# Three of four pairs of the pooling branch's gates made from products of blocks, in a two-layer decoder trunk on one core

## The chip, the cores and the metric

The kernel runs on one core of a Trainium2 chip. Its time is that of one execution on the device, in microseconds; the time of a kernel is the median of its runs. A profile is taken of one further execution. The engines are named as the profile names them: PE multiplies matrices (PEld is its loading of weights), DVE, ACT and POOL work element by element, SP issues transfers (POOL issues some, too).

## What is computed

Two layers, 512 tokens of 1024 features, float32. Each layer has a retention branch and a pooling branch that are merged with gates, then a SwiGLU feed-forward part (FFN). Cut to what matters here:

```
for l in range(DEPTH):                                     # 2
    h = modulate(rmsnorm(x, norm1[l]), sh1, sc1)
    proj = h @ w_in[l]
    q, k, v, g_sw, p_in, gates = jnp.split(proj, IN_SPLITS, axis=-1)
    ...
    ret_d = (jax.nn.silu(g_sw) * ret) @ w_ret_o[l]
    pool_d = (pooled * pool_scale[l]) @ w_pool_o[l]
    a_ret, a_pool = jnp.split(gates, N_BRANCH, axis=-1)
    merged = jax.nn.sigmoid(a_ret) * ret_d + jax.nn.sigmoid(a_pool) * pool_d
    x = x + g1[:, None, :] * (merged @ w_out[l])
    h2 = modulate(rmsnorm(x, norm2[l]), sh2, sc2)
    gate, up = jnp.split(h2 @ w_ffn_in[l], 2, axis=-1)
    x = x + g2[:, None, :] * ((jax.nn.silu(gate) * up) @ w_ffn_out[l])
```

The six modulation vectors of a layer come from `c` and `w_ada`.

## The kernel before, in words

*Layout and precision.* Everything is kept transposed: features on the 128 partitions, the 512 tokens along the row. A tile of 128 features of `h` is therefore 128x512, and `KT` = 8 of them make `h`. Each float32 operand is split into a rounded part and a residue (`hi` and `lo`, both in a reduced float32 type), and `mm3` makes one product from three matmuls: hi by hi, lo by hi, hi by lo. So a column of 128 outputs over all 8 tiles of `h` takes 8 x 3 = 24 matmuls of 512 columns (`project`, line 590).

*Weights.* All weights lie in one stream, `wst`, in chunks of 8 units of 128x128 (512 KB), in the order in which the program asks for them (the table `order`). `ahead(c)` (line 565) prepares chunk c and the two behind it. `prep` (line 504) loads a chunk into one of 3 `raw` tiles and splits it into two of 11 `w` tiles: a copy that rounds (DVE or ACT), and either a subtraction (DVE or POOL) or, for about half of the chunks, a negated copy on ACT and a second transfer that adds the chunk to it (a POOL transfer). The modulation tiles of `w_ada` pass the same 3 `raw` tiles, `background()` (line 634) takes the next of them: one load, and one DVE instruction that multiplies and sums.

*Blocks.* In the FFN, 8 of the 22 pairs of a gate column and an up column (`SEVEN`) are made as a 2 x 2 product of blocks with 7 products of blocks and sums of blocks instead of 8: the two columns are one side, the two halves of the 8 tiles of `h2` the inner side, the two halves of the tokens the other. Each product has 256 columns. `seven_chunk` (line 524) lays the 16 units of a pair into two chunks; `seven_prep` (line 533) loads such a chunk, makes four sums of weight blocks on DVE (256 columns each, into two tiles `r` of 512), and splits the chunk (768 columns of it) and the two tiles of sums: four `w` tiles in all. The sums of `h2` are made once for a layer, into eight pair tiles (`x`). `seven(i)` (line 1047) issues the 84 matmuls into four PSUM tiles (there are 8), and combines these with a copy on ACT and five additions on DVE.

A chunk enters the table `sevens` when its pair is recorded. `ahead` of an earlier column may have reached it before, and has then prepared it as an ordinary chunk; `seven_prep` loads it again.

*The branches.* The retention branch's end (the loop at line 980) goes over 8 columns j: 24 matmuls for the gate, sigmoid, 24 for `ret_o`, the product of the two kept in `m_`, and one modulation tile. The pooling branch's end (line 999) does the same with 24 matmuls for its gate and 12 for `pool_o` (4 tiles of `pooled`), adds `m_[j]`, splits the sum for `w_out`, and takes two modulation tiles. Then come `w_out`'s 8 columns, the second norm, and the FFN.

*What sets the order.* Operations are recorded first (`Recorder`). PE keeps the recorded order; the others are ordered by the times that a planner (`Recorder.order`, line 277) reckons for each engine, by when the result is due, and by when a tile of a pool comes free. `nc.either` leaves the choice of DVE or POOL to it, `copy` that of ACT or DVE. Each engine then runs its list strictly in that order. All instructions are issued at line 421, so a profile tells them apart by the names of their tiles.

Of the kernel before, what the change touches and what calls it, by code (L numbers as in the profile page):

```python
# [14 lines left out]
P = 128  # L15
D = 1024
# [49 lines left out]
SEVEN = [set(range(5, FT - 1, 2))] * DEPTH  # L66
HALF_KT = KT // 2
# [365 lines left out]
def trunk(ctx, tc, xT, cin, wada, vecs, wst, rot, trid, icnt, out):  # L433
# [156 lines left out]
    def project(o, l, name, col, src, sl=FULL, k0=0, mid=None):  # L590
        n = len(src)
        for k in range(n):
            if mid and k == n // 2:
                mid()
            mm3(o[:, sl], unit(l, name, k0 + k, col), hs(src[k], sl), k == 0, k == n - 1)

# [261 lines left out]
    for l in range(DEPTH):  # L858
# [119 lines left out]

        m_ = []
        for j in range(KT):  # L980
            o = ps()
            project(o, l, "in", C_A + j * P, h, mid=head_norm)
            sg = temp()
            nc.scalar.activation(sg, o, AF.Sigmoid)
            while fill:
                filler()
            rp = ps()
            project(rp, l, "ret_o", j * P, y)
            m = keep(F32)
            nc.vector.tensor_mul(out=m, in0=rp, in1=sg)  # L990
            m_.append(m)
            background()
# [3 lines left out]
        for g in (3, 2, 1, 0):  # L996
            group(g)
        pooled = [p2[g] for g in range(4)]
        for j in range(KT):
            gp = ps()  # L1000
            project(gp, l, "in", C_A + D + j * P, h)
            sg = temp()
            nc.scalar.activation(sg, gp, AF.Sigmoid)
            rp = ps()
            project(rp, l, "pool_o", j * P, pooled)
            t = temp()
            nc.vector.tensor_mul(out=t, in0=rp, in1=sg)
            nc.vector.tensor_add(out=t, in0=t, in1=m_[j])
            merged.append(split(t))
            background(2)  # L1010
# [21 lines left out]
        while len(order) % UNITS:  # L1032
            order[("none", len(order))] = len(order)
        done = first_tiles(l, 2, h2, "ffn_in", [0, FF, P], norm_b, block)
        for k in range(HALF_KT):
            t13, t24 = temp(), temp()
            b11, b21, b12, b22 = (block(kk, n) for n, kk in ((0, k), (0, k + HALF_KT), (1, k), (1, k + HALF_KT)))
            nc.either.tensor_sub(out=t13[:, A], in0=b12, in1=b11)
            nc.either.tensor_sub(out=t13[:, B], in0=b12, in1=b22)
            nc.either.tensor_sub(out=t24[:, A], in0=b22, in1=t13[:, A])  # L1040
            nc.either.tensor_sub(out=t24[:, B], in0=b21, in1=t24[:, A])
            hi, lo = sums[k]
            for n, t in enumerate((t13, t24)):
                copy(hi[:, n], t)
                nc.either.tensor_sub(out=lo[:, n], in0=t, in1=hi[:, n].bitcast(F32))

        def seven(i):

            cs = [seven_chunk(l, i, k0) for k0 in (0, 2)]
            o = [ps() for _ in range(4)]  # L1050
            for k in range(HALF_KT):
                ahead(cs[k // 2])
                if k % 2:
                    continue
                (ah, al), (sh, sl) = sevens[cs[k // 2]]

                for (wh, wl), n, bank, at, act in (
                    ((ah, al), 0, 0, 0, "b11"), ((ah, al), 1, 1, 0, "b21"), ((ah, al), 2, 3, 1, 3),
                    ((sh, sl), 2, 1, 1, 2), ((sh, sl), 3, 2, 0, 0), ((sh, sl), 0, 2, 1, 1), ((sh, sl), 1, 3, 0, "b22"),
                ):  # L1060
                    for d in range(2):
                        ws = slice((2 * n + d) * P, (2 * n + d + 1) * P)
                        if isinstance(act, str):
                            a = hs(h2[k + d + HALF_KT * (act[1] == "2")], A if act[2] == "1" else B)
                        else:
                            a = tuple(z[:, act // 2, act % 2 * 256:act % 2 * 256 + 256] for z in sums[k + d])
                        first = k + d == 0 and (bank, at) in ((0, 0), (1, 0), (3, 1), (2, 0))
                        last = k + d == HALF_KT - 1 and (bank, at) in ((0, 0), (1, 1), (2, 1), (3, 0))
                        mm3(o[bank][:, at * 256:at * 256 + 256], (wh[:, ws], wl[:, ws]), a, first, last)
            m1 = temp()[:, A]  # L1070
            nc.scalar.copy(out=m1, in_=o[0][:, A])
            gate, up, u = temp(), temp(), temp()
# [127 lines left out]
```

## Time and profile before

| | us |
|---|---|
| median of 3 runs | 1537.04 (1536.17 to 1537.6) |
| profiled execution: its own time | 1535.18 |
| its span (first to last instruction) | 1533.0 |
| PE, waits for other engines in total | 21 |
| DVE busy | 1006.4 |

The granted clock of PE is full from 100 us on. 286.77 MB are moved in all, 187 GB/s on average. The page's list of DMA issues counts 295 loads of a chunk on SP (4.5 us from issue to landing in the median), 129 on POOL that add to a `w` tile, and 96 loads of modulation tiles on SP.

How to read the rows further on: a timeline row is the start, the time from the first start to the last end of a run of like instructions, the engine, the line, the operation, the tiles (output, arrow, inputs; `w` weights, `h` parts of h or h2, `x` sums of blocks, `r` other activations, `ps` PSUM, `t` temporaries), the shapes and the count; in brackets stands the idle time ahead of it and what ended it. Since matmuls overlap a little, the pace of a stream is read from start to start.

### The profile page before, as it was taken

The numbers are of one execution on the slowest core, as the hardware profiler recorded it, in microseconds if no ns is written. First come the engines' busy times: TensorE is split into PE (matmuls) and PEld (weight loads), VectorE is DVE, ScalarE is ACT, GpSimd is POOL, SyncE is SP. The second block draws the span as 40 slices with busy tenths as digits, with TensorE's granted clock in tenths as the row PEclk, the third lists the DMA queues.
The fourth block names the chain that finished last, engine by engine and source line by source line (L and its number), as shares of the span: only waits on it lengthen the run. The fifth ranks groups of instructions, "written<-read, shape, count | busy, mean of one in ns | idle before, by whom it ended". The sixth has DMA issues, their size and how long they took to land. (4 is left out here: it accounts for less than half of the span.)

```text
span 1533.0 us, 20526 instructions
## 1 busy us (share of the span) xinstructions
PE 1503.3 (98%) x7878; PEld 1287.2 (84%) x7878; DVE 1006.4 (66%) x1650; ACT 645.7 (42%) x912; POOL 300.5 (20%) x291
## 2 busy tenths in 40 slices
PE   7999999999999999999999999999999999999997
PEld 5788888888888888998888888888889888899887
DVE  8877684465568957885366768535647696478633
ACT  2377552322464412342267766322227433243332
POOL 0023151011142300222011312101211432012101
PEclk8999999999999999999999999999999999999999
DMA  7857738789694684559487865777897757444553
GB/s 259 269 158 190 161 74 255 190 246 283 149 234 153 200 251 158 170 169 279 118 221 166 202 149 134 201 180 230 251 232 182 203 167 218 124 130 159 165 125 83
DMA packets 82788, 286.77 MB, mean 187 GB/s; under 512 B 9217, under 2 KB 11521, under 8 KB 82690
## 3 DMA queue, kind: packets, MB, share of 16 engines
q1 hardware_dynamic: 64114, 217.82, 42.5%
q0 software_dynamic: 18576, 67.64, 25.1%
q8 instruction: 61, 1.00, 0.3%
q14 instruction: 37, 0.30, 0.1%
HBM read 283.33 MB, written 2.10 MB: 186 GB/s over the span
## 5 line engine op out<-in xcount | busy, mean ns | idle before, releaser
L421 PE MATMUL ps<-h,w 128*128 128x512 f32 (+1 forms) x3888 | 793.4, 362 | 8.6 <-DVE h L421 5.2
L421 PEld LDWEIGHTS ps<-h,w 128*128 128x128 f32 x3888 | 659.1, 189 | 126.2 <-DVE h L421 6.4
L421 PE MATMUL ps<-r,w 128*128 128x512 f32 (+1 forms) x2430 | 476.8, 356 | 0.1
L421 PEld LDWEIGHTS ps<-r,w 128*128 128x128 f32 x2430 | 402.3, 188 | 69.1 <-DVE r L421 0.9
L421 ACT CAST w<-raw 128x1024 fp32r<-128x1024 f32 (+2 forms) x181 | 183.3, 1013 | 346.9 <-DMA raw<-wst 190.3
L421 DVE TENSOR_TENSOR w<-raw,w 128x1024 fp32r<-128x1024 f32 (+2 forms) x162 | 206.4, 1276 | 102.5 <-PE ps L421 71.7
L421 POOL DMA_DIRECT2D w<-wst x129 | 113.6, 881 | 743.6 <-ACT w L421 690.8
L421 ACT ACTIVATE w<-w 128x1024 fp32r<-128x1024 f32 x129 | 136.6, 1060 | 200.6 <-issue 75.6
L421 DVE CAST w<-raw 128x1024 fp32r<-128x1024 f32 (+2 forms) x115 | 80.4, 699 | 169.0 <-PE ps L421 95.4
L421 DVE SCALAR_TENSOR_TENSOR raw<-raw,cact 128x1024 f32<-128x1024 f32 x96 | 122.5, 1280 | 35.0 <-DMA raw<-wada 33.9
L421 PE MATMUL ps<-x,w 128*128 128x256 f32 x768 | 96.2, 280 | 2.1 <-DVE w L421 2.1
L421 PEld LDWEIGHTS ps<-x,w 128*128 128x128 f32 x768 | 92.8, 188 | 2.5 <-DVE w L421 2.5
L421 PE MATMUL ps<-w,h 128*128 128x512 f32 x384 | 90.3, 395 | 0.0
L421 POOL TENSOR_TENSOR r<-t,r 128x512 fp32r<-128x512 f32 x48 | 79.8, 1669 | 41.1 <-ACT r L421 29.4
L421 PEld LDWEIGHTS ps<-w,h 128*128 128x128 f32 x384 | 72.0, 188 | 17.8 <-ACT r L421 0.4
L421 DVE SCALAR_TENSOR_TENSOR xall<-ps,mod,xall 128x512 f32<-128x512 f32 (+1 forms) x62 | 38.6, 629 | 72.6 <-PE ps L421 72.6
L421 ACT CAST r<-t 128x512 fp32r<-128x512 f32 (+1 forms) x106 | 65.2, 618 | 33.7 <-DVE t L421 25.7
L421 ACT ACTIVATE t<-ps 128x512 f32<-128x512 f32 x76 | 44.9, 593 | 77.8 <-PE ps L421 77.8
L421 DVE TENSOR_TENSOR t<-ps,t 128x512 f32<-128x512 f32 x76 | 51.9, 684 | 15.5 <-PE ps L421 14.6
L421 ACT COPY t<-ps 32x512 f32<-32x512 f32 (+2 forms) x88 | 47.2, 539 | 30.2 <-PE ps L421 20.6
L421 ACT ACTIVATE t<-xall 128x256 f32<-128x256 f32 (+1 forms) x44 | 21.2, 492 | 81.8 <-DVE xall L421 81.5
L421 PE MATMUL ps<-x,r 128*128 128x256 f32 (+2 forms) x256 | 52.7, 323 | 0.0
(93 smaller groups left out, 973.6 us busy)
## 6 DMA issues: line engine op xcount, KB each, us to landing
raw<-wst SPq DMA_DIRECT2D x295, 512.0 KB, 4.5
w<-wst POOLq DMA_DIRECT2D x129, 512.0 KB, 7.5
raw<-wada SPq DMA_DIRECT2D x96, 512.0 KB, 4.8
x<-rot SPq DMA_DIRECT2D x32, 256.0 KB, 7.3
xall<-xT SPq DMA_DIRECT2D x4, 512.0 KB, 5.2
out<-t SPq DMA_DIRECT2D x7, 256.0 KB, 2.2
out<-t SPq DMA_DIRECT2D x2, 128.0 KB, 2.1
tri<-trid SPq DMA_DIRECT2D x1, 128.0 KB, 4.9
```

The costliest lines, as they stand in the source:

```text
L421: getattr(eng, method)(*[real(a) for a in args], **{k: real(v) for k, v in kw.items()})
```

## The change

The pooling branch's gate columns are taken in pairs. Pair 0 (columns 0 and 1) is made as before; pairs 1, 2 and 3 are made by blocks, with the code that was in `seven`, now `block_products`. Behind each pair come its two `pool_o` columns. The sums of h (`make_gate_sums`) are recorded in the first four columns of the retention branch, into the eight pair tiles. The chunks of all block pairs, those of the FFN too, are entered in `sevens` ahead of the columns whose look-ahead reaches them, so that none is prepared as an ordinary chunk first. For that the stream is filled up to a whole chunk ahead of the pooling gates, no longer ahead of the FFN. `seven_prep` makes its three rounding copies on ACT. Of the modulation tiles, two go with each column of the retention branch and one with each of the pooling branch.

```diff
+BLOCK_RET, BLOCK_POOL = (), (1, 2, 3)
...
-    def seven_chunk(l, i, k0):
+    def seven_chunk(l, name, c0, c1, k0):
         c = len(order) // UNITS
-        assert len(order) % UNITS == 0
-        for k, col in ((0, 0), (HALF_KT, 0), (HALF_KT, FF), (0, FF)):
+        assert len(order) % UNITS == 0 and c in sevens
+        for k, col in ((0, c0), (HALF_KT, c0), (HALF_KT, c1), (0, c1)):
             for d in range(2):
-                order[(l, "ffn_in", k + k0 + d, col + i * P)] = len(order)
-        sevens[c] = None
+                order[(l, name, k + k0 + d, col)] = len(order)
         return c
...
-        copy(ah[:, :3 * w], af[:, :3 * w])
+        nc.scalar.copy(out=ah[:, :3 * w], in_=af[:, :3 * w])
...
-            copy(sh[:, part], sf)
+            nc.scalar.copy(out=sh[:, part], in_=sf)
...
+    def block_sums(k, b11, b21, b12, b22, to):
+
+        t13, t24 = temp(), temp()
+        nc.either.tensor_sub(out=t13[:, A], in0=b12, in1=b11)
+        nc.either.tensor_sub(out=t13[:, B], in0=b12, in1=b22)
+        nc.either.tensor_sub(out=t24[:, A], in0=b22, in1=t13[:, A])
+        nc.either.tensor_sub(out=t24[:, B], in0=b21, in1=t24[:, A])
+        hi, lo = to
+        for n, t in enumerate((t13, t24)):
+            copy(hi[:, n], t)
+            nc.either.tensor_sub(out=lo[:, n], in0=t, in1=hi[:, n].bitcast(F32))
+
+    def block_products(l, name, c0, c1, h, sums):
+
+        cs = [seven_chunk(l, name, c0, c1, k0) for k0 in (0, 2)]
+        o = [ps() for _ in range(4)]
...
+        m1 = temp()[:, A]
+        nc.scalar.copy(out=m1, in_=o[0][:, A])
+        gate, up, u = temp(), temp(), temp()
+        nc.vector.tensor_add(out=gate.halves(), in0=o[1].halves(), in1=m1.twice())
+        nc.vector.tensor_add(out=u.halves(), in0=o[2].halves(), in1=gate[:, B].twice())
+        nc.vector.tensor_add(out=gate[:, B], in0=u[:, A], in1=o[3][:, A])
+        nc.vector.tensor_add(out=up[:, A], in0=u[:, B], in1=o[3][:, B])
+        nc.vector.tensor_add(out=up[:, B], in0=u[:, B], in1=o[2][:, A])
+        return gate, up
...
+        for n in BLOCK_POOL:
+            sevens[base + 17 + 3 * n] = sevens[base + 18 + 3 * n] = None
+        gate_sums = [(pair_tile(F32R), pair_tile(F32R)) for _ in range(HALF_KT)]
+
+        def make_gate_sums(k):
+            w = [temp() for _ in range(2)]
+            for t, z in zip(w, (h[k], h[k + HALF_KT])):
+                nc.either.tensor_add(out=t, in0=z[0].bitcast(F32), in1=z[1].bitcast(F32))
+            block_sums(k, w[0][:, A], w[1][:, A], w[0][:, B], w[1][:, B], gate_sums[k])
+
+        def branch(j0, by_blocks, c, mid=None):
+
+            if by_blocks:
+                o = block_products(l, "in", c + j0 * P, c + j0 * P + P, h, gate_sums)
+                for t in o:
+                    nc.scalar.activation(t, t, AF.Sigmoid)
+                yield from enumerate(o, j0)
+                return
...
+                background(2)
+                if j < HALF_KT:
+                    make_gate_sums(j)
...
+        while len(order) % UNITS:
+            order[("none", len(order))] = len(order)
         pooled = [p2[g] for g in range(4)]
...
+        for n in range(HALF_KT):
+            for j, sg in branch(2 * n, n in BLOCK_POOL, C_A + D):
+                rp = ps()
+                project(rp, l, "pool_o", j * P, pooled)
...
+                background()
...
-        while len(order) % UNITS:
-            order[("none", len(order))] = len(order)
+        assert len(order) % UNITS == 0
+        for i in SEVEN[l]:
+            c = len(order) // UNITS + 2 * i + sum(i1 - i0 for i0, i1 in zip(FF_CUTS, FF_CUTS[1:]) if i1 <= i)
+            sevens[c] = sevens[c + 1] = None
```

Where the change moves instructions, first PE, at gate column 2 of layer 0's pooling branch, ahead of it the last product of `pool_o`'s column 1. Before:

```order
L421 MATMUL ps_2685<-r_2608,w_2483 128x512
L421 MATMUL ps_2706<-h_199,w_2483 128x512
L421 MATMUL ps_2706<-h_199,w_2515 128x512
L421 MATMUL ps_2706<-h_222,w_2483 128x512
L421 MATMUL ps_2706<-h_250,w_2483 128x512
L421 MATMUL ps_2706<-h_250,w_2515 128x512
L421 MATMUL ps_2706<-h_307,w_2483 128x512
```

And now, where `w_2600` and `w_2651` are the parts of the chunk itself, with the waits in brackets:

```order
L423 MATMUL ps_2784<-r_2687,w_2575 128x512
L423 MATMUL ps_2811<-h_199,w_2600 128x256
L423 MATMUL ps_2811<-h_199,w_2651 128x256 [waits Pool_49]
L423 MATMUL ps_2811<-h_222,w_2600 128x256
L423 MATMUL ps_2811<-h_250,w_2600 128x256
L423 MATMUL ps_2811<-h_250,w_2651 128x256
L423 MATMUL ps_2811<-h_307,w_2600 128x256
L423 MATMUL ps_2820<-h_410,w_2600 128x256
L423 MATMUL ps_2820<-h_410,w_2651 128x256
```

After two of the eight tiles of `h` the stream goes on to another PSUM tile with other weights of the same chunk; ahead of it the order of PE is that of before. Second, DVE of the changed kernel at the end of pair 1 in the same branch: `raw_2765` is the second chunk of pair 2, `w_2877`, `w_2907` and `w_2947` are residues of pair 2's weights, `ps_2820`, `ps_2852` and `ps_2834` the products of pair 1:

```order
L423 TENSOR_TENSOR w_2877<-r_2786,w_2846 128x512 [waits Activation_49]
L423 TENSOR_TENSOR t_2814<-t_2814,r_2135 128x512
L423 TENSOR_TENSOR w_2907<-raw_2765,w_2880 128x768 [waits PE_49,Activation_49]
L423 TENSOR_TENSOR t_2919<-ps_2820,t_2892 128x512 [waits PE_49,Activation_49]
L423 SCALAR_TENSOR_TENSOR raw_2859,mod_0_150<-raw_2859,cact_73 128x1024 [waits DMAHW0_49,DVE_49]
L423 TENSOR_TENSOR w_2947<-r_2832,w_2914 128x512 [waits PE_49,Activation_49]
L423 TENSOR_TENSOR w_2947<-r_2823,w_2914 128x512 [waits DVE_49,Activation_49]
L423 TENSOR_TENSOR t_2960<-ps_2852,t_2919 128x512 [waits DVE_49,Pool_49]
L423 TENSOR_TENSOR t_2919<-t_2960,ps_2834 128x256 [waits DVE_49,PE_49]
L423 TENSOR_TENSOR t_2969<-t_2960,ps_2834 128x256
```

At that place DVE had one addition and split of a column and two modulation tiles before; now the residues of the next pair stand among the combination of this one, and those of `raw_2765` wait for PE to free their tiles. Third, SP in the second half of layer 0's FFN, from one modulation tile (`wada`) to the next. Before:

```order
L421 DMA raw_5900<-wada 128x1024
L421 DMA raw_5941<-wst 128x1024
L421 DMA raw_5966<-wst 128x1024
L421 DMA raw_5980<-wst 128x1024
L421 DMA raw_6023<-wst 128x1024
L421 DMA raw_6074<-wst 128x1024
L421 DMA raw_6109<-wst 128x1024
L421 DMA raw_6133<-wada 128x1024
```

And now:

```order
L423 DMA raw_5661<-wada 128x1024
L423 DMA raw_5693<-wst 128x1024
L423 DMA raw_5755<-wst 128x1024
L423 DMA raw_5771<-wst 128x1024
L423 DMA raw_5842<-wst 128x1024
L423 DMA raw_5873<-wada 128x1024
```

Two of six loads in each such period are gone.

More of the change, by code (lines that the diff above doesn't have):

```diff
@@ new lines, in block_products @@
+    def block_products(l, name, c0, c1, h, sums):
+        cs = [seven_chunk(l, name, c0, c1, k0) for k0 in (0, 2)]
+        o = [ps() for _ in range(4)]
+        for k in range(HALF_KT):
+            ahead(cs[k // 2])
+            if k % 2:
+                continue
+            (ah, al), (sh, sl) = sevens[cs[k // 2]]
+            for (wh, wl), n, bank, at, act in (
+                ((ah, al), 0, 0, 0, "b11"), ((ah, al), 1, 1, 0, "b21"), ((ah, al), 2, 3, 1, 3),
+                ((sh, sl), 2, 1, 1, 2), ((sh, sl), 3, 2, 0, 0), ((sh, sl), 0, 2, 1, 1), ((sh, sl), 1, 3, 0, "b22"),
+            ):
+                for d in range(2):
+                    ws = slice((2 * n + d) * P, (2 * n + d + 1) * P)
+                    if isinstance(act, str):
+                        a = hs(h[k + d + HALF_KT * (act[1] == "2")], A if act[2] == "1" else B)
+                    else:
+                        a = tuple(z[:, act // 2, act % 2 * 256:act % 2 * 256 + 256] for z in sums[k + d])
+                    first = k + d == 0 and (bank, at) in ((0, 0), (1, 0), (3, 1), (2, 0))
+                    last = k + d == HALF_KT - 1 and (bank, at) in ((0, 0), (1, 1), (2, 1), (3, 0))
+                    mm3(o[bank][:, at * 256:at * 256 + 256], (wh[:, ws], wl[:, ws]), a, first, last)
+        m1 = temp()[:, A]
[7 more added lines that the diff above has]
+        return gate, up
@@ L997, in trunk @@
             group(g)
+        while len(order) % UNITS:
+            order[("none", len(order))] = len(order)
         pooled = [p2[g] for g in range(4)]
[L999 to L1010, printed above, removed]
+        for n in range(HALF_KT):
+            for j, sg in branch(2 * n, n in BLOCK_POOL, C_A + D):
+                rp = ps()
+                project(rp, l, "pool_o", j * P, pooled)
+                t = temp()
+                nc.vector.tensor_mul(out=t, in0=rp, in1=sg)
+                nc.vector.tensor_add(out=t, in0=t, in1=m_[j])
+                merged.append(split(t))
+                background()
         mods_done(l, 40)
@@ L1029, in trunk @@
         norm_b = close(l, "out", 0, merged, 16, STAT_TILES["out"], half_a)
-        while len(order) % UNITS:
-            order[("none", len(order))] = len(order)
+        assert len(order) % UNITS == 0
+        for i in SEVEN[l]:
+            c = len(order) // UNITS + 2 * i + sum(i1 - i0 for i0, i1 in zip(FF_CUTS, FF_CUTS[1:]) if i1 <= i)
+            sevens[c] = sevens[c + 1] = None
         done = first_tiles(l, 2, h2, "ffn_in", [0, FF, P], norm_b, block)
         for k in range(HALF_KT):
[L1036 to L1045, printed above, removed]
@@ L1047, in seven @@
-        def seven(i):
[L1049 to L1072, printed above, removed]
-            nc.vector.tensor_add(out=gate.halves(), in0=o[1].halves(), in1=m1.twice())
-            nc.vector.tensor_add(out=u.halves(), in0=o[2].halves(), in1=gate[:, B].twice())
-            nc.vector.tensor_add(out=gate[:, B], in0=u[:, A], in1=o[3][:, A])
-            nc.vector.tensor_add(out=up[:, A], in0=u[:, B], in1=o[3][:, B])
-            nc.vector.tensor_add(out=up[:, B], in0=u[:, B], in1=o[2][:, A])
@@ L1078, in seven @@
+            block_sums(k, *(block(kk, n) for n, kk in ((0, k), (0, k + HALF_KT), (1, k), (1, k + HALF_KT))), sums[k])
+        def seven(i):
+            gate, up = block_products(l, "ffn_in", i * P, FF + i * P, h2, sums)
             nc.scalar.activation(gate, gate, AF.Silu)
```

29 lines of the change are left out of this document (16 added, 13 removed).

## The prediction

> **What bounds the kernel now.** I read the page's busy times first, then the waits of PE, then PE's timeline in the two stages that the change touches, and last DVE there.
>
> ```profile
> span 1533.0 us, 20526 instructions
> PE 1503.3 (98%) x7878; PEld 1287.2 (84%) x7878; DVE 1006.4 (66%) x1650; ACT 645.7 (42%) x912; POOL 300.5 (20%) x291
> ```
>
> PE is busy for 98% of the span, so the time is the length of PE's stream plus its few waits. DVE, at 66% on average, matters only where it is fuller than that. In the list of what PE waited for, two rows bear on this case:
>
> ```profile
> PE ps L421 <- DVE acc L421: 2.7, 2, 2.3
> PE ps L421 <- DVE w L421: 2.1, 2, 1.3
> ```
>
> The first is a norm between stages; the order of DVE's work at those places stays the same, so I leave it. The second, PE waiting for DVE to finish a weight tile (w), is in the blocks of the FFN, and the change touches it.
>
> PE's timeline in the pooling branch of layer 0 (start, duration, tiles, shape, count):
>
> ```profile
> 304.00 5.66 PE L421 MATMUL ps<-h,w 128*128 128x512 f32 x24
> 309.50 2.91 PE L421 MATMUL ps<-r,w 128*128 128x512 f32 x12
> 312.24 5.66 PE L421 MATMUL ps<-h,w 128*128 128x512 f32 x24
> ```
>
> From start to start a gate column of 24 products of 512 takes 309.50 - 304.00 = 5.50 us (229 ns each), its pool_o column of 12 takes 2.74 us, and nothing stands in brackets: PE doesn't wait here. Now the FFN of layer 0, where every second column pair is already made by 7 products of blocks:
>
> ```profile
> 618.77 2.99 PE L421 MATMUL ps<-x,w 128*128 128x256 f32 x24
> 621.60 2.28 PE L421 MATMUL ps<-h,w 128*128 128x256 f32 x18
> 623.72 2.99 PE L421 MATMUL ps<-x,w 128*128 128x256 f32 x24
> 626.54 13.28 PE L421 MATMUL ps<-h,w 128*128 128x256 f32 x66
> 639.66 2.99 PE L421 MATMUL ps<-x,w 128*128 128x256 f32 x24
> ```
>
> From 618.77 to 639.66 lies one block pair and one ordinary pair (the row of 66 holds the block's last 6 products, the 48 ordinary ones, and 12 of the next block): 20.89 us. One run of 24 products of 256 columns takes 2.83 us, 118 ns each, about half of 229.
>
> **The change, part by part.**
>
> *Products.* An ordinary pair of gates is 2 x 24 = 48 products of 512 columns: 2 x 5.50 = 11.0 us. A block pair is 84 products of 256: 20.89 - 11.0 = 9.9 us. One pair saves 1.1 us (10.98 - 9.91 = 1.07 unrounded); 3 pairs in each of 2 layers make **-6.4 us**. It lies on PE, which has no slack, so it all counts.
>
> [...]
>
> *Double loads in the FFN.* Before, a chunk of a block pair became known as such only when the pair was recorded, so the look-ahead of two chunks had already loaded and split it as an ordinary one. The order shows 32 fewer loads of 512 KB on SP, two for each of the 16 FFN pairs, with their two conversions each. What this cost PE is in layer 1:
>
> ```profile
> 1242.44 2.99 PE L421 MATMUL ps<-x,w 128*128 128x256 f32 x24
> 1247.38 2.40 PE L421 MATMUL ps<-x,w 128*128 128x256 f32 x19
> 1250.58 0.86 PE L421 MATMUL ps<-x,w 128*128 128x256 f32 x5 [0.80 <-DVE w L421]
> ...
> 1264.40 2.99 PE L421 MATMUL ps<-x,w 128*128 128x256 f32 x24
> ...
> 1269.34 2.40 PE L421 MATMUL ps<-x,w 128*128 128x256 f32 x19
> 1273.03 0.86 PE L421 MATMUL ps<-x,w 128*128 128x256 f32 x5 [1.28 <-DVE w L421]
> ```
>
> The period from 1242.44 to 1264.40 is 21.96 us, 1.07 more than the undisturbed 20.89. In the next, 19 products should take 2.24 us and take 1273.03 - 1269.34 = 3.69: 1.45 lost. The chain of waits ahead of it:
>
> ```profile
> 1256.73 2.26 DVE raw L421 x2
> 1259.00 4.20 DMA raw<-wst
> ...
> 1272.37 0.61 DVE w L421
> ```
>
> The block's second chunk was fetched only at 1259.00, when a raw tile came free, and its last residue was done at 1272.98, 14 us later. Six weight loads pass the three raw tiles in each period there, and now four. DVE, too, loses up to two conversions of a copy and a subtraction per period. Bounds: nothing, if DVE's other work sets this chain, or all of it. The nearest row with less load is the second half of layer 0's FFN (below), with no wait at all, so I take all: **-2.5 us**.
>
> *Work that DVE, ACT and POOL gain.* A chunk of a block needs four sums of 256 columns and three splits where an ordinary one needs one split; each pair needs five combinations out of PSUM; each layer four sets of sums of h. The groups of before, shapes kept apart (busy, mean ns of one):
>
> ```profile
> L421 DVE TENSOR_TENSOR t<-ps,t 128x512 f32<-128x512 f32 x76 | 51.9, 684 | 15.5 <-PE ps L421 14.6 <-ACT t L421 0.7
> L421 DVE SCALAR_TENSOR_TENSOR raw<-raw,cact 128x1024 f32<-128x1024 f32 x96 | 122.5, 1280 | 35.0 <-DMA raw<-wada 33.9 <-issue 0.7
> L421 DVE TENSOR_TENSOR w<-raw,w 128x768 fp32r<-128x768 f32 x32 | 35.0, 1095 | 4.8 <-ACT w L421 3.1 <-PE ps L421 1.4
> L421 DVE TENSOR_TENSOR w<-r,w 128x512 fp32r<-128x512 f32 x61 | 43.5, 718 | 6.7 <-ACT w L421 2.5 <-PE ps L421 1.7
> L421 DVE TENSOR_TENSOR r<-raw 128x256 f32<-128x256 f32 x64 | 31.1, 522 | 5.9 <-DMA raw<-wst 5.9
> L421 DVE TENSOR_TENSOR w<-raw,w 128x1024 fp32r<-128x1024 f32 x128 | 170.3, 1331 | 97.7 <-PE ps L421 70.3 <-issue 13.2 <-ACT w L421 10.7
> L421 DVE TENSOR_TENSOR t<-t,ps 128x256 f32<-128x256 f32 x48 | 18.6, 417 | 1.0
> L421 DVE TENSOR_TENSOR r<-r,raw 128x256 f32<-128x256 f32 x32 | 15.6, 486 | 0.0
> L421 DVE TENSOR_TENSOR r<-raw,r 128x256 f32<-128x256 f32 x32 | 13.4, 419 | 0.1
> L421 DVE TENSOR_TENSOR t<-t,r 128x512 f32<-128x512 f32 x21 | 17.1, 815 | 0.3
> L421 DVE TENSOR_TENSOR r<-t,r 128x512 fp32r<-128x512 f32 x44 | 32.5, 740 | 4.0 <-ACT r L421 3.3
> L421 DVE CAST r<-t 128x512 fp32r<-128x512 f32 x34 | 14.5, 425 | 1.7 <-POOL t L421 0.8
> L421 ACT CAST w<-raw 128x768 fp32r<-128x768 f32 x29 | 24.3, 836 | 55.8 <-DMA raw<-wst 52.1 <-DVE w L421 2.9 <-PE ps L421 0.7
> L421 ACT CAST w<-r 128x512 fp32r<-128x512 f32 x18 | 10.8, 619 | 21.8 <-DVE r L421 15.0 <-PE ps L421 4.9 <-DVE w L421 1.8
> ```
>
> In the new order of layer 0, DVE has between the first combination of pair 1 and that of pair 2, in the order of the rows above: 4 x 0.684 + 2 x 1.280 + 2 x 1.095 + 3 x 0.718 + 4 x 0.522 + 1.331 + 3 x 0.417 + 2 x 0.486 + 2 x 0.419 = 16.1 us. Counted the same way the next turn has 13.0. PE's turn is 9.9 + 2 x 2.74 = 15.4 us. So DVE is some 94% full for three turns. How full it was, and whether PE waited, is in the windows (span, then PE, PEld, DVE, ACT, POOL busy):
>
> ```profile
> 215.20:304.00 88.80, 88.53 (x385) 72.34 (x386) 43.06 (x60) 25.92 (x33) 15.30 (x17) 1.00 0.74 201
> 304.00:367.20 63.20, 63.20 (x278) 51.86 (x277) 43.21 (x68) 14.55 (x20) 12.06 (x11) 1.00 0.89 256
> 596.00:712.00 116.00, 116.00 (x712) 104.02 (x711) 96.59 (x150) 41.83 (x55) 23.18 (x19) 1.00 0.59 185
> 1221.50:1285.40 63.90, 61.82 (x386) 55.49 (x385) 59.42 (x83) 27.86 (x37) 24.79 (x13) 1.00 0.56 175
> ```
>
> The pooling branch of before is at 43.2 of 63.2 us, 68%. The FFN at 83% shows no wait; at 59.4 of 63.9 us, 93%, it shows the two waits above. This is the unknown of the change: what full turns of DVE cost PE. Two deadlines:
>
> - A chunk's four weight tiles. There are 11; two block chunks and a pool_o chunk hold 10. So the next pair's first chunk gets its tiles when PE has used the same chunk of the pair before, half a block (4.95 us) in, and is needed 4.95 + 5.49 = 10.4 us later. What stands on that path, end to end: ACT 0.836 + 2 x 0.619 = 2.1, DVE 1.095 + 2 x 0.718 = 2.5, and ahead of them in DVE's queue the combination (2 x 0.684 + 3 x 0.417), two multiplications by the gate (2 x 0.684) and a modulation tile (1.280): 5.3. Together 9.9 us: it fits, by half a microsecond if nothing overlapped. The subtraction that waits for its tile holds up everything behind it on DVE, the combination first of all, which frees PSUM banks; but the next block begins with the banks freed earliest.
> - The last merged tile. After the last pool_o column DVE needs 0.684 + 0.815 + 0.425 + 0.740 = 2.7 us, and w_out's first column reaches that tile after 21 of its 24 products, 21 x 0.229 = 4.8 us.
>
> Bounds for the new waits: 0, as at 83%, and 6 x 1.26 = 7.6 us, if each of the six pairs waits like the two of layer 1's FFN (1.07 and 1.45). The load is nearest to the row with waits, but there a late load began the chain, and here the order puts a pair's conversions a whole turn ahead. I take a quarter of it, **+2 us**.
>
> The sums of h (four sets in a layer; by rows of the same shapes 2 x 0.69 + 4 x 0.42 + 2 x 0.43 + 2 x 0.74 = 5.4 us each, an estimate) and eight modulation tiles (8 x 1.28 = 10 us) go to the retention branch, whose window is the first row above: 43.1 of 88.8 us, and some 75 with both. DVE's room there hides them: cost nothing. The modulation tiles leave the pooling branch, one for each column, 10 us of DVE and 8 loads, which pays for the raw tiles that blocks hold longer. With that cover gone, the rival of starving pairs below is what it would cost. The combination's copies and the forced copies on ACT are 2.1 us for a chunk, 4.2 in a turn of 15.4: nothing.
>
> Sum: -6.4 - 2.5 + 2.0 = -6.9 us. The profiled run took 1535.18 us, 2.18 beyond its span; so a span of 1526.1 and a run of 1528.3. The median of the runs shown is 1537.04, 1.86 above the profiled one: **1530.1 us**.
>
> **The rivals.**
>
> - *Everything hides.* New waits are 0, and the remaining short waits (the longest for acc, 2.3 us, among them) shrink by luck of the order by 1 to 2: 1537.0 - 8.9 - 1.5 = 1526.6. For it: the deadlines above fit. Against: DVE at 94%.
> - *Pairs starve.* Each pair waits 1.26 us, 7.6 in all; FFN waits go by half: 1537.0 - 6.4 - 1.2 + 7.6 = 1537.0, and with two thirds of that 1534.5. No change, within what can be measured.
> - *Conversions start only with the free tiles* (slower). If a chunk's load, too, can't begin before tiles come free, since its raw tile is held by the chunk ahead, the chain of 14.0 us seen above stands against 10.4 us: 3.6 us late for pairs 2 and 3 of each layer, 14 us. 1537.0 - 8.9 + 14.4 = 1542.5. It decides once the chain exceeds 10.4 us. Against it: the order issues both loads of a pair next to each other, a turn ahead.
> - *Weights bind the small products* (slower). A block pair loads weights 84 times for 48. The profile has one load as
>
> ```profile
> L421 PEld LDWEIGHTS ps<-x,w 128*128 128x128 f32 x768 | 92.8, 188 | 2.5 <-DVE w L421 2.5
> ```
>
>   and if each extra load of 188 ns stood in the stream, a pair would pay 36 x 0.188 = 6.8 us and lose 5.7; six pairs 34 us: 1569. The rows of the FFN speak against it: 118 ns from product to product, so that a load of 188 ns must overlap its neighbours. The Trainium skill speaks for it ("TensorE: Matmul & The Clock Gate", in "Part 3: Packing small matmuls", under "What overlaps and what doesn't"): a weight load is to overlap running matmuls only where it goes to other row groups of the array, while these use all rows. By that rule blocks would lose; the trace disagrees, 118 ns being under one load.
> - *The change doesn't do what it says*: the order shows 288 fewer products of 512, 504 more of 256 and 32 fewer loads, so this is out.
>
> **How the numbers follow.** About 0.2%, 3.1 us, is what a measurement of this kernel can tell from no change. Chances: forecast, with new waits of 0.5 to 4 us (1528.5 to 1532.5), 0.62; everything hides 0.13; pairs starve 0.18, of which I count 0.11 as within 0.2% and 0.07 as faster; late conversions 0.06; bound weights 0.01. Faster 0.62 + 0.13 + 0.07 = 0.82, same 0.11, slower 0.07. The range from 1526.5 to 1535.0 takes in the forecast, half of the hiding case and over half of the starving one: 0.62 + 0.07 + 0.10, or 0.79.
>
> **What would show it.** In the profile after, the pooling branch should be 63.2 - 3 x 1.07 = 60.0 us long, each block 9.9 us, with 118 ns between products; PE's waits for w in the FFN of layer 1 should be gone; DVE in the pooling branch should be above 85%. Right sum for a wrong reason would be FFN waits that stay and no waits in the pooling branch. It is wrong if rows in brackets stand at the heads of blocks or at w_out's first column, for w or ps, above 4 us in all.

## The result, and the profile after

| | before | after |
|---|---|---|
| median beside the first profile of after | 1535.91 (7 runs) | 1524.86 (7 runs, 1524.37 to 1531.2) |
| ratio, 95% interval | | 0.9945 (0.9929 to 0.996) |
| profiled execution, its span | 1535.18, 1533.0 | 1530.62, 1528.9 |
| chunk loads on SP | 295 | 263 |

The changed kernel is faster, by some 0.55%. Its median lies 5.2 us below the 1530.1 predicted. Its single runs spread widely, and the profiled one is among the slowest, so that the profiles differ by 4.6 us and the medians by 11; the first experiment takes that up.

The blocks of the pooling branch first: the timeline of PE, layer 0, then layer 1 (`...` stands for rows left out).

```profile
324.03 1.52 PE L423 MATMUL ps<-h,w 128*128 128x256 f32 x12
...
333.55 5.66 PE L423 MATMUL ps<-r,w 128*128 128x512 f32 x24
339.04 1.52 PE L423 MATMUL ps<-h,w 128*128 128x256 f32 x12
...
1070.67 1.58 PE L423 MATMUL ps<-h,w 128*128 128x256 f32 x12
...
1080.57 5.67 PE L423 MATMUL ps<-r,w 128*128 128x512 f32 x24
1086.07 1.58 PE L423 MATMUL ps<-h,w 128*128 128x256 f32 x12
```

No row has a bracket: PE waits for nothing at the heads of blocks. A block takes 9.90 us in layer 1, as forecast, but 9.52 in layer 0: 84 products at 113.3 ns instead of 117.8. How full VectorE (DVE) is, by the windows (length, then PE, PEld, DVE, ACT and POOL busy, PE's granted clock, DMA share, GB/s) of the retention branch's end, the pooling branch, and layer 1's FFN:

```profile
215.40:307.50 92.10, 88.77 (x385) 72.25 (x386) 72.19 (x91) 28.82 (x39) 38.71 (x33) 1.00 0.78 221
307.55:366.30 58.75, 58.75 (x385) 53.31 (x384) 48.14 (x89) 26.72 (x41) 11.25 (x10) 1.00 0.62 186
1216.00:1280.00 64.00, 64.00 (x404) 57.84 (x403) 45.34 (x74) 25.21 (x35) 8.01 (x6) 1.00 0.50 160
```

Over the pooling branch DVE is at 82%; in the three turns of a block and its two `pool_o` columns it is busy for 13.0, 12.5 and 11.2 of 15.0 us, where the prediction has 94%. The branch is 58.75 us long from its first gate to its last `pool_o` column, against 60.0 forecast, since layer 0's blocks run at 113.3 ns here. In the FFN DVE went from 59.4 of 63.9 us to 45.3 of 64, and the two waits for `w` are gone; where PE's timeline of before breaks into 19 and 5 products, it now has:

```profile
1246.07 2.99 PE L423 MATMUL ps<-x,w 128*128 128x256 f32 x24
...
1266.95 2.99 PE L423 MATMUL ps<-x,w 128*128 128x256 f32 x24
```

The retention branch's end, though, has 92.1 us where 88.8 stood, and PE is busy for only 88.8 of them. Its head in PE's timeline:

```profile
216.23 0.50 PE L423 MATMUL ps<-r,ones_r 128*128 128x512 f32 x1 [1.10 <-DVE r L423]
216.57 2.92 PE L423 MATMUL ps<-h,w 128*128 128x512 f32 x12
219.32 4.97 PE L423 MATMUL ps<-r,w 128*128 128x512 f32 x21
226.52 0.73 PE L423 MATMUL ps<-r,w 128*128 128x512 f32 x2 [2.22 <-ACT r L423]
227.54 0.50 PE L423 MATMUL ps<-r,w 128*128 128x512 f32 x1 [0.29 <-DVE r L423]
```

Before, the only wait here was 0.31 us; now the three come to 3.6. In layer 1 the waits at this place are those of before (0.67 and 0.33 us). The last head's activations are late, and DVE's and GpSimd's (POOL's) rows of the time just ahead show why:

```profile
219.38 1.74 POOL L423 TENSOR_TENSOR r<-t,r 128x512 fp32r<-128x512 f32 x1
219.88 1.25 DVE L423 TENSOR_TENSOR r<-t,ic 128x2 f32<-128x2 f32 x1
221.08 2.40 POOL L423 TENSOR_TENSOR w<-raw,w 128x1024 fp32r<-128x1024 f32 x1
221.17 2.33 DVE L423 TENSOR_TENSOR r<-r,t 128x2 f32<-128x2 f32 x1
223.42 0.68 DVE L423 SCALAR_TENSOR_TENSOR t<-t,t 128x512 f32<-128x512 f32 x1
```

Two operations on two columns take 1.25 and 2.33 us. The first ends with POOL's operation that runs until 221.12, the second with POOL's subtraction of weights, which runs from 221.08 to 223.48. Before, they took 0.15 and 0.16 us with the same shapes:

```profile
219.58 0.15 DVE L421 TENSOR_TENSOR r<-t,ic 128x2 f32<-128x2 f32 x1
219.77 0.16 DVE L421 TENSOR_TENSOR r<-r,t 128x2 f32<-128x2 f32 x1
...
223.87 2.31 DVE L421 TENSOR_TENSOR w<-raw,w 128x1024 fp32r<-128x1024 f32 x1
```

There the subtraction of the weights stood on DVE, behind the head's chain. The Trainium skill ("SBUF — State Buffer", in "SBUF: two separate sides") has DVE and GpSimd share one pair of ports under an exclusive lock: of a DVE operation with two operands in SBUF and a GpSimd instruction that reads SBUF, the one that starts first keeps the ports until it is over. The trace agrees: 2.33 us beside POOL, 0.16 without. (The first wait, 1.10 us for 0.31, is not of this kind: DVE's list has one more operation ahead of the result that PE waits for.)

### The profile page after: what moved, and what is told of

Same layout as the page of the kernel before. It is cut to its first block, busy times and chain, and to the rows that moved or that the text cites. A ratio compares the mean times of both kernels' runs of the same rounds, so it can differ in the third digit from the quotient of the medians.

```text
span 1528.9 us, 21049 instructions
## 1 busy us (share of the span) xinstructions
PE 1496.6 (98%) x8094; PEld 1293.4 (85%) x8094; DVE 1023.6 (67%) x1729; ACT 677.6 (44%) x983; POOL 289.8 (19%) x283
## 4 chain that ended last, share of the span: by engine, by line
PE 91%; DVE 4%; DMA 3%; ACT 1%; issue 1%; POOL 0%; DVEq 0%; ACTq 0%; SPq 0%; POOLq 0%
PE ps L423 91%; DMA raw<-wst 2%; DVE t L423 1%; DVE w L423 1%; DMA w<-wst 1%; DVE raw L423 1%; DVE r L423 1%; ACT w L423 0%; DMA xall<-xT 0%; ACT t L423 0%; ACT r L423 0%; DVE acc L423 0%; POOL w L423 0%; DVE h L423 0%; ACT h L423 0%
## 5 line engine op out<-in xcount | busy, mean ns | idle before, releaser
L423 PE MATMUL ps<-h,w 128*128 128x512 f32 (+1 forms) x3816 | 753.6, 356 | 6.6 <-DVE h L423 4.8
L423 PEld LDWEIGHTS ps<-h,w 128*128 128x128 f32 x3816 | 632.8, 189 | 112.0 <-DVE h L423 5.5
L423 DVE TENSOR_TENSOR w<-raw,w 128x1024 fp32r<-128x1024 f32 (+2 forms) x136 | 165.4, 1217 | 115.0 <-PE ps L423 86.8
L423 DVE CAST w<-raw 128x1024 fp32r<-128x1024 f32 (+1 forms) x88 | 62.7, 713 | 109.8 <-PE ps L423 67.6
L423 PE MATMUL ps<-x,w 128*128 128x256 f32 x1056 | 130.9, 279 | 0.0
L423 PEld LDWEIGHTS ps<-x,w 128*128 128x128 f32 x1056 | 126.8, 188 | 0.0
L423 ACT CAST w<-r 128x512 fp32r<-128x512 f32 x88 | 51.8, 620 | 86.4 <-PE ps L423 51.0
L423 POOL TENSOR_TENSOR w<-r,w 128x512 fp32r<-128x512 f32 x17 | 29.4, 1729 | 270.6 <-PE ps L423 150.7
L423 DVE TENSOR_TENSOR w<-r,w 128x512 fp32r<-128x512 f32 x71 | 49.0, 721 | 26.3 <-PE ps L423 17.4
L423 DVE TENSOR_TENSOR r<-t,r 128x512 fp32r<-128x512 f32 (+1 forms) x84 | 57.8, 691 | 8.5 <-ACT r L423 7.2
```

Source lines behind the costliest of these rows:

```text
L423: getattr(eng, method)(*[real(a) for a in args], **{k: real(v) for k, v in kw.items()})
```

## The experiments

Theory T is the prediction's sum, with one correction from the profile: some 3 us of new waits at the retention branch's head, put down to the sums of h. Its rivals: the gain is that of the loads made once (R1), or the products give all of it (R2). All medians and ratios are against runs of the kernel before on the same chip.

### The changed kernel again, and what makes runs differ

Edit: none.

> The changed kernel once more, unaltered, since its runs fell at two levels 5.6 us apart (about 1524.7 and 1530.4) and its profile was of the upper one. Theory T (the sum of the prediction; waits at the end of layer 0's retention branch cost some 3 us in the profile): the gain against before stays at 0.994 to 0.996, and a profile at the lower level has the same new waits at the head of the retention branch's end (some 3.3 us for r), so that what it lacks lies elsewhere. Rival W: the levels are these very waits, which come in some executions and not in others; then a lower profile has none of them. Rival C (clock and pace): the levels are a stretch at half the clock (1.7 us lost in the profile) and the pace of the 256-column products, 113.3 or 117.8 ns (1056 + 504 of them by 4.4 ns are up to 6.9 us); then a lower profile has longer stretches at 113.3.

> The changed kernel once more, unaltered, beside the kernels of this batch. Theory C: reduced in the same way it comes out within 0.5 of 1292.1, 8 us below before, its waits for r at layer 0's retention branch are 1.1 and 2.1 us again, and its median is 0.994 to 0.996 of before. Rival V: the reduced span is over 1.5 us away.

> The kernel before, unaltered, for a second profile of it. Theory C (single runs differ by the pace of the products, short half-clock stretches and the start-up): reduced to the fastest paces seen (113.3 and 228.9 ns), without half-clock stretches and from the retention branch's start on, the first profile of before gives 1300.1 us, the two of the changed kernel 1292.0 and 1292.2; this one then comes out within 0.5 of 1300.1, whatever its time, with the waits for w (1.1 and 1.5 us) in layer 1's FFN. Rival V (the waits themselves vary from run to run): more than 1.5 us away from it.

Measured: after again 1526.79 us (8 runs), ratio 0.9954 (0.9936 to 0.9971), and the third time 1528.51 (12 runs, 1519.41 to 1534.49), ratio 0.9959 (0.994 to 0.9979). Before again: 1534.47 (12 runs, 1531.07 to 1538.15), ratio 1.0002. All three profiles of after have the waits at the retention branch's head (1.10 and 2.08 to 2.22 us), though their times are 1530.62, 1524.94 and 1533.74: rival W, by which these waits make the levels, is out. What differs is the pace. Counted over all starts of matmuls, a product of 256 columns begins either 113.3 or 117.8 ns after the one ahead, one of 512 either 228.9 or 233.3; a pace holds over whole blocks and stages. Layer 1's FFN, from the end of its norm (1166.40 us in the first profile) to the start of the kernel's last product, takes 353.96 us in the first profile of after, at 117.8 ns, and 350.40 in the second, at 113.3. Then there are half-clock stretches of 3.4 us, such as this one behind the wait for `acc` at the start of layer 0's FFN, in the first profile of after (a window; 0.53 is the granted clock):

```profile
420.20:423.60 3.40, 3.40 (x17) 3.31 (x16) 2.40 (x7) 2.71 (x4) 0.00 (x0) 0.53 0.09 13
```

From 200 us on the three profiles of after have 1, 3 and 3 of these, at some 1.7 us each (half of 3.4), the two of before 0 and 1. Last, the retention branch's end starts between 209 and 215 us in the profiles.

So from here on a **reduced span** stands beside the medians: the span from the first gate product of layer 0's retention branch's end on, less what every product of 256 or 512 columns starts late by, at the slower pace or at half the clock, against 113.3 or 228.9 ns behind the one ahead. Waits stay in. Before has 1308.7 and 1308.6, after 1301.5, 1301.6 and 1301.4. (The expectations quote 1300.1 for before and 1292.0 to 1292.2 for after, reduced in another way that is not on record, so only differences compare: 8 us there, 7.2 here.) It repeats within 0.2 us, so theory C holds, rival V is out, and after is 7.2 us below before.

All kernels in that measure:

| kernel | median, us (runs) | ratio to before, 95% | reduced span |
|---|---|---|---|
| before | 1534.47 (12) | 1.0002 (0.9988 to 1.0016) | 1308.7, 1308.6 |
| after | 1526.79 (8), 1528.51 (12) | 0.9954, 0.9959 | 1301.5, 1301.6, 1301.4 |
| no blocks in the pooling branch | 1534.09 (12) | 0.9996 (0.9979 to 1.0013) | 1309.0 |
| FFN chunks loaded twice | 1527.35 (10) | 0.9953 (0.9936 to 0.9971) | 1302.0 |
| copies to either engine | 1529.98 (12) | 0.997 (0.9956 to 0.9983) | 1301.5 |
| both of these | 1531.77 (12) | 0.9979 (0.9966 to 0.9992) | 1303.2 |
| modulation tiles as before | 1543.55 (8) | 1.0053 (1.0035 to 1.0072) | 1310.4 |
| the same, four raw tiles | 1562.76 (4) | 1.0186 (1.0164 to 1.0208) | 1317.0 |
| modulation tiles late | 1526.52 (12) | 0.9949 (0.9932 to 0.9966) | 1298.9 |
| modulation tiles later | 1523.63 (6) | 0.9925 (0.9907 to 0.9942) | 1296.7 |
| late, four pairs | 1534.82 (12) | 1.0005 (0.9983 to 1.0027) | 1304.4 |

### Without the blocks of the pooling branch

```diff
-BLOCK_RET, BLOCK_POOL = (), (1, 2, 3)
+BLOCK_RET, BLOCK_POOL = (), ()
-        gate_sums = [(pair_tile(F32R), pair_tile(F32R)) for _ in range(HALF_KT)]
...
-                if j < HALF_KT:
-                    make_gate_sums(j)
```

> The pooling gates by plain products again and no sums of h; all else as after (chunks of the FFN declared ahead, copies on ScalarE, modulation tiles moved). Theory T: the products are worth 6.4 us (six pairs by 1.07) and the sums of h cost some 3 us at the end of layer 0's retention branch, so this is 3 to 4 us slower than after and 2.5 to 3.5 us faster than before: 1528; a pooling branch of 63.2 us, and no 2.2 us wait for r at the retention branch's end. Rival R1 (the gain is that of the loads made once and of the moved tiles, the products give nothing): as after, 1524.9 within 1 us. Rival R2 (products give all): as before, 1535.9.

Measured: 1534.09, the time of before, and 7.3 us above the after of the same chip; by the reduced span 7.5. The stage from the first pooling gate to `w_out` takes 65.92 us here and 62.64 in the second profile of after, both at 117.8 ns: 1.09 us per pair, against 1.07 forecast. R1 is out. By its number R2 is right, yet not as it was meant: the rest of the change does two things that cancel. Layer 1's FFN has lost its waits, and the retention branch's head has them: 1.10 and 2.06 us for `r`, here without any sums of h. So T's cause for these, the sums, is wrong, and its time of 1528 was missed.

### The waits in the FFN: loads made once, or copies on ScalarE

Three kernels: the loop over `SEVEN` that enters the chunks ahead left out (loads twice, 295 of them); the copies back on either engine; both.

```diff
-        for i in SEVEN[l]:
-            c = len(order) // UNITS + 2 * i + ...
-            sevens[c] = sevens[c + 1] = None
...
-        nc.scalar.copy(out=ah[:, :3 * w], in_=af[:, :3 * w])
+        copy(ah[:, :3 * w], af[:, :3 * w])
...
-            nc.scalar.copy(out=sh[:, part], in_=sf)
+            copy(sh[:, part], sf)
```

> As after, but the chunks of the FFN's blocks aren't declared ahead, so that 32 of them are loaded twice as before (295 loads). Theory T: the two waits for w in the FFN of layer 1 return, 2.5 us: 1527.4. Rival R1 (the loads made once carry most of the gain): 5 us or more slower than after, 1530 or above. Rival H: VectorE's queue is shorter for another reason (copies on ScalarE), so the waits don't return and the time is that of after within 1 us.

> As after, but the three copies that round a block chunk's combinations go to whichever engine the planner takes, as before, not always to ScalarE; loads are still made once. Theory A (loads made once or copies on ScalarE each suffice against the waits for w in layer 1's FFN): no waits, that FFN stage 354.0 us at 117.8 ns between products, 350.4 at 113.3, as after within 1 us. Theory B (the copies alone remove them): the waits return, the stage is some 3 us longer, 357.2 or 353.5.

> As after, with both undone: copies to whichever engine the planner takes, and the FFN's block chunks loaded twice (295 loads). Theories A and B: the waits for w in layer 1's FFN return, as in the kernel before (stage 357.2 us at 117.8 ns), 2.5 to 3.1 us slower than after. Rival N (neither: the waits went because of a shift of the order at the FFN's start, as the new place of the modulation tiles): no waits, as after within 1 us.

Measured: 1527.35 with the loads twice, as after; 1529.98 with the copies back, and 1531.77 with both. Only the last has the waits again, in PE's timeline of layer 1's FFN at the places where before has 0.80 and 1.28:

```profile
1243.41 2.40 PE L423 MATMUL ps<-x,w 128*128 128x256 f32 x19
1246.44 0.86 PE L423 MATMUL ps<-x,w 128*128 128x256 f32 x5 [0.64 <-DVE w L423]
...
1264.96 2.32 PE L423 MATMUL ps<-x,w 128*128 128x256 f32 x19
1268.60 0.86 PE L423 MATMUL ps<-x,w 128*128 128x256 f32 x5 [1.33 <-DVE w L423]
```

The other two pass the same stage without a wait. So theory A holds: either edit alone is enough. The copies' median lies 1.5 to 3.2 us above after's, which ran on other chips; the reduced span (1301.5) shows none of it, and its cause stays open.

### The modulation tiles back in their places

```diff
-                background(2)
+                background()
                 if j < HALF_KT:
...
-                background()
+                background(2)
```

> As after, but the modulation tiles stand where they stood before (one for each column of the retention branch's end, two for each of the pooling branch). Theory T: with fewer large operations of GpSimd and VectorE at the retention branch's end the waits for r there (1.1 + 2.2 us) shrink by 1 to 3 us, while VectorE in the pooling branch of 60 us gets 10 us more, near full, and waits for w appear there, 1 to 5 us: in sum within 2 us of after. Rival M: the waits for r come from the sums of h alone and stay as they are, and the pooling branch has room: as after within 0.5 us. Rival S (pairs starve): 4 us or more slower, with waits at the heads of the blocks.

Measured: 1543.55, slower than before. The waits at the retention branch's head are gone (0.31 us is left, the stage takes 88.63 us), which puts their cause on the moved tiles. The price is at the end of the pooling branch, in PE's timeline of layer 0 and layer 1:

```profile
365.07 12.09 PE L423 MATMUL ps<-r,w 128*128 128x512 f32 x40 [3.82 <-DMA w<-wst]
...
1120.77 4.51 PE L423 MATMUL ps<-r,w 128*128 128x512 f32 x10 [4.87 <-DMA w<-wst]
```

Each runs into a half-clock stretch of 6.8 us, twice the usual length. What PE waits for is the second product's weights in the `pool_o` chunk behind the last block: POOL's transfer that completes them. POOL issues it at 356.59 in layer 0, where it lands at 365.02, and in layer 1, where it lands at 1120.73, with this row:

```profile
1111.97 0.88 POOL L423 DMA_DIRECT2D w<-wst  x1 [5.86 <-ACT w L423]
```

SP's queue in layer 0 shows why that chunk is late (issues of chunks `raw<-wst` and of modulation tiles `raw<-wada`; first this kernel, then after):

```profile
338.03 9.05 SPq L423 DMA_DIRECT2D raw<-wada  x4
349.60 4.01 SPq L423 DMA_DIRECT2D raw<-wst  x3
355.11 8.53 SPq L423 DMA_DIRECT2D raw<-wada  x4
365.66 0.33 SPq L423 DMA_DIRECT2D raw<-wst  x1
```

```profile
340.30 5.04 SPq L423 DMA_DIRECT2D raw<-wada  x2
345.46 6.58 SPq L423 DMA_DIRECT2D raw<-wst  x3
352.23 3.07 SPq L423 DMA_DIRECT2D raw<-wada  x2
357.12 13.79 SPq L423 DMA_DIRECT2D raw<-wst  x4
```

The chunk's own load is the first of the three issued from 349.60 on, 45.9 us behind the start of the pooling branch (303.70). In after it is issued at 345.46, 37.9 us behind that start (307.55). Here four modulation tiles stand ahead of it in the queue, in after two; each needs one of the three raw tiles and keeps it until DVE has read it. T's "within 2 us of after" is missed and rival M is out; S has the time, but not the place, since no block waits at its head. To tell the raw tiles from a full DVE, the same with a fourth raw tile (and two temporary tiles fewer, for room):

```diff
-N_RAW, N_W, N_X, N_H, N_ROW, N_TEMP = 3, 11, 8, 2 * KT, 28, 9
+N_RAW, N_W, N_X, N_H, N_ROW, N_TEMP = 4, 11, 8, 2 * KT, 28, 7
```

> As the kernel with the modulation tiles back in their old places (two for each pooling column), but with four raw tiles instead of three for what is loaded, and seven temporary tiles instead of nine to make room. That kernel waited 3.8 and 4.9 us for w at the end of the pooling branch, behind which came half-clock stretches of 6.8 us. Theory W4 (modulation tiles hold the raw tiles, so that weight chunks are loaded late): these waits shrink to less than half, and the time falls by 5 us or more towards that of after. Rival D (VectorE is full, by 10 us more work in 60): the waits stay or turn into waits for DVE, and the time stays within 3 us of 1543 or rises; fewer temporary tiles may add to it in either case.

Measured: 1562.76, 19 us more where 5 less were expected. The two waits shrink to less than half, as W4 has it: from 3.82 to 1.26 us and from 4.87 to 1.18. The load of that chunk is issued 41.1 us behind the start of the pooling branch instead of 45.9, and the stage in layer 0 goes from 69.33 to 63.93 us. Most of the added time is pace: from the retention branch's end on, the products of 512 columns lose 16.9 us at the slower pace in this profile, 1.8 with three raw tiles. By the reduced span the kernel is 6.6 us slower, and a wait of 4.92 us for `acc` at the end of layer 0's `w_out`, which after doesn't have, is part of it. Whether that comes of the missing temporary tiles or of the fourth raw tile was not separated. So the time misses W4's figure, while the waits bear out its mechanism, the late loads.

### The modulation tiles later in the retention branch

```diff
-                background(2)
+                background((1, 1, 2, 2, 2, 2, 3, 3)[j])
```

and, in a second kernel, `(0, 1, 2, 2, 2, 3, 3, 3)`.

> As after, but of the 16 modulation tiles that the retention branch's end gets, the first two columns take one each and the last two three each (1, 1, 2, 2, 2, 2, 3, 3 for 2 in every column). Theory T2: the waits for r at the start of that branch in layer 0 (1.1 + 2.1 + 0.3 us) come from the tiles of the first columns, with which VectorE's queue looks so full to the planner that the weight subtraction goes to GpSimd, beside which the 128x2 operations of the head's chain are held; here they go, the stage from the branch's start to the pooling branch is 88.6 us again (after: 91.3 and 92.9), and a half-clock stretch behind it goes with them where there was one: 3 to 5 us faster than after. Rival Q (the sums of h make these waits): the waits stay, as after within 1 us. Rival L (three tiles in the last columns hold loads and raw tiles): waits of 3 us or more for a load of w at the pooling branch, slower than after.

> As after, with the retention branch's modulation tiles moved further back than in the kernel with 1, 1, 2, 2, 2, 2, 3, 3: 0, 1, 2, 2, 2, 3, 3, 3 for its eight columns. That one still had a wait of 1.2 us. Theory T2: with none in the first column the weight subtraction stays on VectorE behind the head's chain, no wait of over 0.4 us is left there, the stage up to the pooling branch is 88.6 us, and the reduced span is 2.7 us below that of after: 1289.4; the median 2 to 4 us below that of after on this chip. Rival Q (sums of h): a wait of 1 us or more stays. Rival L (three tiles in each of the last columns hold up loads): waits for w at the pooling branch, time as after or above.

Measured: late 1526.52, later 1523.63, both with all sums of h where they were. In the first the two-column operations take 0.15 and 0.16 us again, but POOL still has the weight subtraction, and now a larger operation is caught beside it, and PE behind that:

```profile
220.88 2.84 POOL L423 TENSOR_TENSOR w<-raw,w 128x1024 fp32r<-128x1024 f32 x1
222.15 2.11 DVE L423 TENSOR_TENSOR r<-t,r 128x512 fp32r<-128x512 f32 x1 [0.69 <-ACT r L423]
224.32 0.50 PE L423 MATMUL ps<-r,w 128*128 128x512 f32 x1 [1.20 <-DVE r L423]
```

So the stage is 89.7 us there, and T2's 88.6 is missed. In the second kernel the subtraction is back on DVE, behind the chain, and no wait above 0.31 us is left at the head:

```profile
220.70 1.03 DVE L423 TENSOR_TENSOR r<-t,r 128x512 fp32r<-128x512 f32 x1 [0.69 <-ACT r L423]
221.66 2.31 DVE L423 TENSOR_TENSOR w<-raw,w 128x1024 fp32r<-128x1024 f32 x1
```

The stage is 88.63 us long, and the reduced span falls by 4.8 us against after, more than the 2.7 expected (the wait for `w` behind the last block of layer 1 is gone, too): T2 holds, Q and L don't. In its batch this kernel's six runs all lie between 1521.8 and 1524.5, while the changed kernel has 1528.51; its ratio of 0.9925 (0.9907 to 0.9942) against 0.9959 (0.994 to 0.9979) makes it the fastest tried, though the intervals touch, and after's other two (0.9945 and 0.9954) overlap more. The stage without waits and the reduced span carry the finding.

### Four pairs instead of three

```diff
-BLOCK_RET, BLOCK_POOL = (), (1, 2, 3)
+BLOCK_RET, BLOCK_POOL = (), (0, 1, 2, 3)
```

on top of the tiles late (1, 1, 2, 2, 2, 2, 3, 3).

> As the kernel with the tiles late (1, 1, 2, 2, 2, 2, 3, 3), and all four pairs of the pooling gates by products of blocks. Theory T: two more pairs by 1.07 us (1.45 at 113 ns): 2.1 to 2.9 us faster than three pairs, no new waits. Rival P: the first pair's conversions come in the stretch where VectorE still does sums of h and modulation tiles, so that its block waits for w at its head, 1 to 4 us in each layer: same as three pairs or slower.

Measured: 1534.82 (1525.54 to 1543.19), 8 us slower than three pairs. Against rival P the first block waits for nothing; against T, waits for POOL's transfers of `pool_o` chunks come behind blocks, as with the tiles back (PE's timeline of layer 0; the last row is a wait for DVE):

```profile
333.57 5.55 PE L423 MATMUL ps<-r,w 128*128 128x512 f32 x23 [1.17 <-DMA w<-wst]
366.08 9.43 PE L423 MATMUL ps<-r,w 128*128 128x512 f32 x40 [1.45 <-DMA w<-wst]
376.33 26.65 PE L423 MATMUL ps<-r,w 128*128 128x512 f32 x152 [0.82 <-DVE r L423]
```

So a fourth pair of chunks that need four `w` tiles each doesn't fit with the rest as it is. The reduced span is 5.5 us longer than with three pairs; which of raw tiles, `w` tiles and queue ends last there was not tried.

## Why the prediction was right, point by point

- **The products (-6.4 us): right.** 1.09 us per pair at 117.8 ns, where 1.07 was forecast, and 1.47 where both paces are the fast ones (2 x 24 x 228.9 ns less 84 x 113.3). Taking the blocks out costs 7.3 to 7.5 us, net of the wait behind layer 1's last block, below.
- **The double loads (-2.5): right in sum, half right in cause.** The two waits of layer 1's FFN went, 2.1 us in the first profile of before and 1.5 in the second, and the stage is 2.1 to 3.1 us shorter at one pace. But loading once is enough without being needed: with the loads doubled and the copies on ACT the waits stay away. I had set the copies at nothing, since ACT has room; that they unload DVE, at 93% there, I passed over.
- **New waits in the pooling branch (+2): mis-sized, and of another kind.** No block waits at its head, and PE waits for nothing of DVE's. The count in the order gave DVE 16.1 and 13.0 us in two turns; the fullest turn has 13.0 of 15.0. What there is, 0.42, 1.75 and 0.58 us in the three profiles, is a wait for POOL's transfer of the `pool_o` chunk behind the last block of layer 1.
- **Sums of h and modulation tiles in the retention branch ("cost nothing"): the step that failed.** They have room in sum, as forecast: 72 of 92 us, where I had reckoned 75 of 88.8. But not at the branch's head in layer 0, where the last head's chain is still on PE's path: with two tiles per column the planner gives the weight subtraction to POOL, DVE's operations beside it are held, and PE waits 3.3 us longer than before, plus up to 1.7 where a half-clock stretch follows. The runs show which part it was: the tiles in the first columns, not the sums. I had bounded this move by busy shares over 89 us and not by the deadline of the chain at their start.
- **The modulation tiles leave the pooling branch, "which pays for the raw tiles": right, and worth more than the text made of it.** Without that move the change is slower than before, by 0.35 to 0.72%.
- **The rivals.** Pairs do not starve with three blocks. With four, or with the tiles back, PE waits behind blocks, by late loads, which is nearest to the rival "conversions start only with the free tiles". Bound weights are out: products start 113.3 to 117.8 ns apart with loads of 188 ns.
- **The base.** The forecast of 1530.1 rests on 1537.04, a median of three runs. In 25, 35 and 23 further runs before has 1534.0 to 1534.6. So the base is some 2.5 us of the 5.2 by which the median lay lower; the ratio forecast, 1530.1 / 1537.04 or 0.9955, is what the runs gave (0.9945 to 0.9959). By parts, in reduced spans: products -8.8 (6 x 1.47), FFN -2.1 to -3.1, retention head +3.1, the wait behind layer 1's last block +0.4 to +1.7, for -7.2 measured. That the sum of -6.9 comes so near is in part luck: the +2 put on the pooling branch stands in for the 3.1 us at the retention head, which had been put at nothing, and the products gain more at the fast pace than was counted.

## What to carry to other kernels

Work that "fits" a stage by its busy share can still be late at one end of it: look for the chain that PE waits for next, and put moved work behind it, not just into the same stage. Where a scheduler chooses between two engines that hold each other up, adding work to one changes the other's list, and a two-column operation can then cost as much as a large one. And where single runs spread by several microseconds, reduce the profiles to the waits and the work before comparing them; three runs are too few for a base.

## What the runs showed of the hardware

- Matmuls have two paces 4.44 ns apart, 113.3 and 117.8 ns for 256 columns, 228.9 and 233.3 for 512, at the same full granted clock; one holds over whole stages. Which one differs between executions of one program: the first profile of after has 268 of its 3226 products of 256 columns at the fast pace, the second 1844 of 3229, 7.0 us. The program has a part in it, too: with four raw tiles and seven temporary ones, 94% of the products of 512 columns are at the slower pace, and 10 to 32% in all other profiles. What decides it stays open. The Trainium skill ("TensorE: Matmul & The Clock Gate", "Back-to-back issue gap") lists one gap for a width, that of an isolated matmul: 262 cycles for 256 columns and 518 for 512.
- A short wait can cost a half-clock stretch of 3.4 us, and so up to 1.7 us more. From 200 us until the last products, every such stretch in the profiles begins in a wait or within 1.4 us of its end: waits of 1.1 and 2.1 us ten microseconds apart (in two of three profiles of after), single ones of 1.7 to 2.5 us (in some), and with 6.8 us those of 3.5 to 4.9. The Trainium skill (the same page, "HAM oscillation — how this bites in real kernels") names gaps of over some 3.4 us; here shorter ones were enough.
